# Splitting weights three tiles ahead in the last stage of a decoder layer

## The chip, the core and the metric

The kernel runs on one core of a Trainium2 chip. The metric is the time of one execution on the device, in microseconds (us), median of the runs shown. PE is the matrix engine, PEld its weight loads, DVE the vector engine, ACT the scalar engine, POOL the GpSimd engine, and SP the engine whose queue issues most DMAs.

## The reference

One decoder layer for a prompt of 1024 tokens and 64 sample tokens (8 sequences of 8), width 1024, all in fp32: a feed-forward half, a mixing part (forgetting attention beside gated linear attention), and a second feed-forward half. Only the second feed-forward half matters here:

```python
def swiglu(x, w_gu, w_down):
    gate, up = jnp.split(x @ w_gu, 2, axis=-1)
    return (jax.nn.silu(gate) * up) @ w_down

def macaron_half(x, g_pre, w_gu, w_down, g_post):
    return x + 0.5 * rmsnorm(swiglu(rmsnorm(x, g_pre), w_gu, w_down), g_post)
```

The hidden width is 2752: 21 blocks of 128 and a tail of 64.

## The kernel before, in words

All 1088 tokens lie in columns, the model dimension on partitions (8 slices of 128). A matrix product in fp32 accuracy is made of three products in a faster format: each operand is split into a high part and a low remainder, and high x high, high x low and low x high are summed in PSUM. `split` makes the parts: ACT casts the source to the high part (L192), DVE subtracts it from the source to give the low part (L193). For weights the source is a raw tile of 128x1024 (or 128x512), and the parts are called `wh` and `wl`.

`Feed` brings the weights. It holds one list of requests in the order in which jobs use them. A request is loaded into a raw tile (`wr`, two buffers, L117), split into `wh` and `wl` (three buffers each, `NW` = 3), and handed to its job by `get`. `free` says that a job has used its tiles, and calls `pump`, which writes further splits and loads: the splits up to `freed + ahead` tiles, and `ahead` is `NW - 1` = 2 where no caller says otherwise. So while job j is written, the tiles of j and j+1 are split. `work` goes through the jobs: get, pump, run the job, free.

The second feed-forward half runs twice: once for the first 512 tokens, and then, as the last stage of the kernel, for the other 576 (Part `f3`, begun by the job `start5`). This last stage makes the hidden blocks 2 to 19 in groups of 4, 4, 4, 4 and 2 ("sevens"). For each hidden block, gate and up products together would be 8 quarter products (two column halves of tokens by two halves of the contraction, for gate and for up); they are made with 7, after Winograd's form of Strassen's method. Each quarter product is 4 slices x 3 matmuls of 288 columns, in one PSUM tile. The operands of the 7 are sums of gate and up weights, which `Sums.load` makes for each block: tiles x (`wx`), y, z (`wz`) and s4. DMAs bring the raw parts, and POOL makes three sums for x and y (L89) and one for s4 (L94). x, y, z and s4 are the four tiles of the block's four jobs (`job_seven`, i = 0 to 3), with 2, 2, 2 and 1 products. Tile y, s4 and one raw part live in the memory of the first 512 tokens' result, which must have been written out first (`old3`).

The products are evacuated from PSUM by ACT (the first of a block, L581) or DVE (L565): sums of products give gate and up. After a block, ACT applies silu (L574), DVE multiplies by up (L575), and ACT and DVE split the result into `hh` and `hl` (L577, L578). In the last block of a group these steps are done for each half of the tokens apart. Then come the group's four down products (L495), each with one tile of `in_wd`, evacuated by DVE (L505). PSUM gives the products three tiles (`mm`) and one more for every fourth of a block (`mx`).

Within the sevens the flag `kept` makes ACT and DVE keep the order in which the code writes their instructions; elsewhere the framework's scheduler may reorder. After the sevens come the last two hidden blocks and their down products ("last"), and the final norm.

Of the kernel before, what the change touches and what calls it, by code (L numbers as in the profile page):

```python
# [31 lines left out]
NW = 3  # L32
# [35 lines left out]
class Sums:  # L68


    def __init__(self, gate, up, f, first=None):
        self.gate, self.up, self.f = gate, up, f
        self.i = 0 if first is None else first.count
        self.first = first or self
        self.first.count = self.i + 1
# [22 lines left out]
class Feed:  # L98


    def __init__(self, step, reqs):
        self.step, self.reqs = step, reqs
        self.raws, self.parts = [], []
        self.taken = self.freed = 0

    def _raw(self):
        s, nc = self.step, self.step.nc
        req = self.reqs[len(self.raws)]
        if isinstance(req, Sums):
            self.raws.append(req.load(s))  # L110
            return
        t = s.W.tile([P, KB * P], F32, name=s.uid("wr"), tag="wraw", bufs=NRAWW)
        pieces, _ = req
        o = 0
        for p in pieces:
            n = p.shape[-1]
            nc.sync.dma_start(t[:, o:o + n], p)  # L117
            o += n
        self.raws.append((t, o))
# [14 lines left out]
        s.split(hi[:, :n], lo[:, :n], t[:, :n])  # L134
        self.parts.append((hi, lo))

    def pump(self, ahead=NW - 1):
        while len(self.parts) < min(len(self.reqs), self.freed + ahead):
            self._split()
        while len(self.raws) < min(len(self.reqs), len(self.parts) + NRAWW):  # L140
            self._raw()
        while len(self.raws) < min(len(self.reqs), len(self.parts) + NSUMS) and isinstance(self.reqs[len(self.raws)], Sums):
            self._raw()
# [4 lines left out]
        self.taken += 1  # L148
        return self.parts[self.taken - 1]

    def free(self, n=1, ahead=NW - 1):
        self.freed += n
        self.pump(ahead)

# [989 lines left out]
class StepB(StepA):  # L1144
# [423 lines left out]
    def whole(self):  # L1568
# [158 lines left out]

        def start5():
            p4.close()
            f3.H, _ = self.pool("H2", keep=True)  # L1730
            self.px, _ = self.pool("px", keep=True, space=PSUM)
        norm0 = self.norm(y, 0, *CH[0], F, pre=0, key="f1", v=[self.rms_quick(y, CH[0][1], F)])
        next(norm0)
        jobs.append(([], start5, 0))
        jobs += self.ffn(A["wgu2"], A["wd2"], f3)
        self.work(jobs)
# [96 lines left out]
```

## Time and profile before

| | us |
|---|---|
| median of 3 runs | 2414.66 (2413.93 to 2417.48) |
| profiled execution | 2405.93 |
| its span, first to last instruction | 2404.2 |
| PE busy | 2300.9 (96%) |
| DVE, ACT, POOL busy | 1282.9, 899.8, 474.7 |

The mean granted clock of the matrix engine was 0.985 of full speed. In the span, the last stage with its first blocks starts near 1965 us; the first product of the sevens runs at 2004.5, the last near 2330, and the rest is the last two blocks and the norm.

How the rows read: in order of time, a row gives start, duration, engine, line, operation, output<-inputs, shape and count, and in brackets how long the engine sat idle before it and what ended that. A row of stretches gives for each engine the busy time, and then the granted clock, the share of the DMA engines and GB/s. Busy times of merged rows overlap, since instructions are pipelined.

### The profile page before, as it was taken

To read this page: it belongs to the slowest core of one execution; us is meant where nothing else is said; L and a number is where in the kernel's file an instruction comes from. 1 tells how busy PE (TensorE), PEld (TensorE's weight loads), DVE (VectorE), ACT (ScalarE), POOL (GpSimd) and SP (SyncE) were. 2 spreads that over 40 slices of the span, in tenths; PEclk is the share of its full clock that TensorE was granted. 3 is DMA by queue.
4 is the path that set the end of the run, shared out by engine and by line. 5 is a ranking of instruction groups with operands and counts; after the bars stand their busy time and mean duration, and the time that the engine had idled before them with its cause. 6 is when DMAs were issued, how large, how long until landed. Compare 5 with 4: busy or idle time off the path is not lost. (4 is left out here: it accounts for less than half of the span.)

```text
span 2404.2 us, 39346 instructions
## 1 busy us (share of the span) xinstructions
PE 2300.9 (96%) x15200; PEld 2041.1 (85%) x15200; DVE 1282.9 (53%) x2453; ACT 899.8 (37%) x1622; POOL 474.7 (20%) x514
## 2 busy tenths in 40 slices
PE   7999999999999999999998999999997999999997
PEld 7999999999989879899996666677777998999997
DVE  7223232232347775776464333358885786667655
ACT  5411211111134555755454212236465544333322
POOL 4000000000003230011134454611100324223302
PEclk9999999999999999999999999999998999999998
DMA  3211111111135577664458998755654534222212
GB/s 123 71 44 45 44 45 44 46 49 48 45 97 158 165 226 210 183 189 144 125 185 280 321 332 291 252 159 165 167 167 142 183 117 155 86 86 91 77 53 91
DMA packets 182268, 330.55 MB, mean 137 GB/s; under 512 B 25730, under 2 KB 101315, under 8 KB 182083
## 3 DMA queue, kind: packets, MB, share of 16 engines
q1 hardware_dynamic: 170418, 289.77, 38.7%
q0 software_dynamic: 11664, 38.28, 4.6%
q8 instruction: 120, 1.97, 0.3%
q14 instruction: 66, 0.53, 0.1%
HBM read 284.29 MB, written 43.69 MB: 136 GB/s over the span
## 5 line engine op out<-in xcount | busy, mean ns | idle before, releaser
L263 PE MATMUL mm<-ua,wh 128*128 128x512 f32 (+2 forms) x2288 | 636.6, 365 | 4.8 <-ACT ua L405 2.0
L263 PE MATMUL mm<-ub,wh 128*128 128x256 f32 (+2 forms) x2624 | 544.9, 303 | 10.4 <-ACT ub L192 8.0
L193 DVE TENSOR_TENSOR wl<-wr,wh 128x1024 fp32r<-128x1024 f32 (+1 forms) x258 | 312.6, 1212 | 339.4 <-ACT wh L192 337.4
L192 ACT CAST wh<-wr 128x1024 fp32r<-128x1024 f32 (+1 forms) x258 | 263.4, 1022 | 573.0 <-PE mm L263 220.7
L263 PEld LDWEIGHTS mm<-ua,wh 128*128 128x128 f32 (+1 forms) x2288 | 401.4, 192 | 80.8 <-issue 22.4
L263 PEld LDWEIGHTS mm<-ub,wh 128*128 128x128 f32 (+1 forms) x2624 | 427.2, 191 | 17.6 <-ACT ub L192 8.2
L263 PE MATMUL mm<-ua,wl 128*128 128x512 f32 (+1 forms) x1136 | 406.3, 359 | 0.9 <-DVE wl L193 0.9
L263 PE MATMUL mm<-ub,wl 128*128 128x256 f32 (+1 forms) x1296 | 385.9, 298 | 0.3 <-DVE wl L193 0.3
L495 PE MATMUL mm<-hl,wh 128*128 128x256 f32 (+2 forms) x1088 | 346.9, 320 | 0.0
L495 PE MATMUL mm<-hh,wh 128*128 128x256 f32 (+2 forms) x1040 | 336.9, 325 | 7.9 <-ACT wh L192 4.3
L495 PE MATMUL mm<-hh,wl 128*128 128x256 f32 (+2 forms) x1040 | 331.7, 320 | 2.1 <-DVE wl L193 2.1
L263 PEld LDWEIGHTS mm<-ub,wl 128*128 128x128 f32 x1296 | 247.7, 191 | 0.5 <-DVE wl L193 0.5
L263 PEld LDWEIGHTS mm<-ua,wl 128*128 128x128 f32 x1136 | 217.2, 192 | 33.0 <-DVE wl L193 2.0
L505 DVE TENSOR_TENSOR y<-y,mm 128x256 f32<-128x256 f32 (+2 forms) x272 | 130.3, 504 | 192.6 <-PE mm L495 191.5
L495 PEld LDWEIGHTS mm<-hh,wh 128*128 128x128 f32 x1040 | 196.0, 189 | 26.9 <-issue 6.2
L495 PEld LDWEIGHTS mm<-hl,wh 128*128 128x128 f32 x1088 | 206.0, 189 | 12.6 <-issue 1.3
L277 POOL TENSOR_TENSOR ss<-ss,sq 128x256 f32<-128x256 f32 (+1 forms) x46 | 46.2, 1005 | 834.1 <-ACT sq L273 833.5
L495 PEld LDWEIGHTS mm<-hh,wl 128*128 128x128 f32 x1040 | 196.1, 189 | 15.2 <-DVE wl L193 3.1
L961 POOL DMA_INDIRECT pr<-in_cv,rows x128 | 128.5, 1004 | 114.6 <-PE po L1038 60.2
L433 DVE TENSOR_TENSOR sg<-mm,sg 128x256 f32<-128x256 f32 (+4 forms) x76 | 39.3, 517 | 132.7 <-PE mm L263 130.7
L192 ACT CAST hh<-sg 128x512 fp32r<-128x512 f32 (+2 forms) x92 | 47.0, 511 | 156.3 <-DVE sg L433 134.4
L550 PE MATMUL mm<-ub,wh 128*128 128x288 f32 x432 | 89.0, 297 | 3.9 <-ACT y L503 3.9
(290 smaller groups left out, 3187.8 us busy)
## 6 DMA issues: line engine op xcount, KB each, us to landing
wr<-in_wgu SPq DMA_DIRECT2D x101, 512.0 KB
wr<-in_wd SPq DMA_DIRECT2D x60, 512.0 KB
pr<-in_ck SPq DMA_DIRECT2D x112, 256.0 KB
wr<-in_win SPq DMA_DIRECT2D x50, 512.0 KB
wr<-in_wout SPq DMA_DIRECT2D x32, 512.0 KB
wz<-in_wgu SPq DMA_DIRECT2D x36, 256.0 KB
h<-y SPq DMA_DIRECT2D x12, 512.0 KB
x<-h SPq DMA_DIRECT2D x24, 256.0 KB
```

The lines of the kernel that those rows point to most:

```text
L192: self.keep(self.nc.scalar.copy(hi, src))
L193: self.keep(self.nc.vector.tensor_tensor(out=lo, in0=src, in1=hi.bitcast(F32), op=ALU.subtract))
L263: nc.tensor.matmul(out, a, x[:, k, o:o + n], start=(k == 0 and j == 0), stop=(k == KB - 1 and j == len(ops) - 1))
L277: (nc.gpsimd if odd else nc.vector).tensor_tensor(out=s, in0=s, in1=sq[:, :n], op=ALU.add)
L433: nc.vector.tensor_tensor(out=out, in0=u, in1=t, op=ALU.mult)
L495: nc.tensor.matmul(pds[e], a, b, start=(i == 0 and j == 0), stop=(i == len(g) - 1 and j == len(ops) - 1))
L505: nc.vector.tensor_tensor(out=yk, in0=yk, in1=pds[e], op=ALU.add)
L550: nc.tensor.matmul(ps, a, x, start=(k == 0 and j == 0), stop=(k == KB // 2 - 1 and j == len(ops) - 1))
L961: nc.gpsimd.indirect_dma_start(out=raw[:, i], out_offset=None, in_=A["ck" if kind == "K" else "cv"].rearrange("g p n -> (g p) n"), in_offs ...
```

## The change

`Feed` gets a field `ahead`, 2 at first. `pump` and `free` use it where the caller gives no number. `start5` sets it to 3, so that from the last stage on the splits reach three tiles ahead: while job j is written, tile j+2 is split as well, into the buffers that job j-1 used.

```diff
@@ class Feed
         self.taken = self.freed = 0
+        self.ahead = NW - 1
...
-    def pump(self, ahead=NW - 1):
+    def pump(self, ahead=None):
+        ahead = ahead or self.ahead
         while len(self.parts) < min(len(self.reqs), self.freed + ahead):
             self._split()
...
-    def free(self, n=1, ahead=NW - 1):
+    def free(self, n=1, ahead=None):
         self.freed += n
         self.pump(ahead)
...
         def start5():
             p4.close()
+            self.feed.ahead = NW
```

It changes the order of instructions on each engine, and their number on none. Lines of the changed kernel are higher by 1 to 3.

DVE, second block of a group, before (`y<-y,mm` with number 20621 evacuates the block's second product, `wl<-wz` is the split of tile z, `wl<-y` with 128x512 that of s4, `wl<-y` with 128x1024 that of y):

```order
L565 TENSOR_TENSOR sg_20477<-y_7670,mm_20579 128x288
L193 TENSOR_TENSOR wl_20594<-y_7670,wh_20593 128x1024
L565 TENSOR_TENSOR y_7670<-y_7670,mm_20621 128x288
L575 TENSOR_TENSOR sg_20477<-sg_20477,up_20478 128x576
L193 TENSOR_TENSOR wl_20639<-wz_20461,wh_20638 128x1024
L565 TENSOR_TENSOR y_7670<-y_7670,mm_20642 128x288
L565 TENSOR_TENSOR y_7670<-y_7670,mx_20655 128x288
L565 TENSOR_TENSOR up_20607<-y_7670,mx_20655 128x288
L578 TENSOR_TENSOR hl_20470<-sg_20477,hh_20469 128x576
L193 TENSOR_TENSOR wl_20674<-y_7670,wh_20673 128x512
L565 TENSOR_TENSOR sg_20606<-y_7670,mm_20678 128x288
L565 TENSOR_TENSOR up_20607<-y_7670,mm_20691 128x288
```

The same place now:

```order
L567 TENSOR_TENSOR sg_20481<-y_7670,mm_20592 128x288
L195 TENSOR_TENSOR wl_20607<-wz_20430,wh_20606 128x1024
L567 TENSOR_TENSOR y_7670<-y_7670,mm_20625 128x288
L577 TENSOR_TENSOR sg_20481<-sg_20481,up_20482 128x576
L195 TENSOR_TENSOR wl_20643<-y_7670,wh_20642 128x512
L567 TENSOR_TENSOR y_7670<-y_7670,mm_20647 128x288
L567 TENSOR_TENSOR y_7670<-y_7670,mx_20660 128x288
L567 TENSOR_TENSOR up_20611<-y_7670,mx_20660 128x288
L580 TENSOR_TENSOR hl_20474<-sg_20481,hh_20473 128x576
L195 TENSOR_TENSOR wl_20679<-wx_20583,wh_20678 128x1024
L567 TENSOR_TENSOR sg_20610<-y_7670,mm_20682 128x288
L567 TENSOR_TENSOR up_20611<-y_7670,mm_20695 128x288
```

In each of the four slots for a split now stands the split of the next tile: z where y stood, s4 where z stood, the next block's x where s4 stood.

ACT, end of a group, before (`wh<-wr` are the casts of the group's first and second down weights, `sg<-sg` the silu of each half, `hh<-sg` the casts of the gated halves):

```order
L192 CAST wh_20928<-y_7670 128x512
L574 ACTIVATE sg_20859<-sg_20859 128x288
L577 CAST hh_20475<-sg_20859 128x288
L192 CAST wh_20966<-wr_20895 128x1024
L574 ACTIVATE sg_20859<-sg_20859 128x288
L577 CAST hh_20475<-sg_20859 128x288
L192 CAST wh_20990<-wr_20932 128x1024
```

The same place now:

```order
L194 CAST wh_20897<-y_7670 128x512
L579 CAST hh_20477<-sg_20741 128x576
L194 CAST wh_20934<-wr_20863 128x1024
L576 ACTIVATE sg_20865<-sg_20865 128x288
L579 CAST hh_20479<-sg_20865 128x288
L194 CAST wh_20972<-wr_20901 128x1024
L576 ACTIVATE sg_20865<-sg_20865 128x288
L579 CAST hh_20479<-sg_20865 128x288
```

Each cast of down weights moved ahead of the silu and the cast of one half. DVE's halves of these splits moved in the same way: that of the second down weights now stands ahead of the evacuation of the stage's last product.

SP's queue at the stage's start, before (`x<-h` and `out_yT<-y` belong to the output of the first 512 tokens, `y<-in_wgu` is a raw part for the first block's sums):

```order
L117 DMA wr_20271<-in_wd 128x512
L366 DMA x_24239<-h_87 128x2x320
L386 DMA out_yT<-y_7670 128x4x256
L366 DMA x_24241<-h_87 128x2x320
L386 DMA out_yT<-y_7670 128x4x256
L86 DMA y_7670<-in_wgu 128x512
L117 DMA wr_20895<-in_wd 128x1024
L117 DMA wr_20932<-in_wd 128x1024
```

The same place now:

```order
L118 DMA wr_20275<-in_wd 128x512
L118 DMA wr_20863<-in_wd 128x1024
L368 DMA x_24239<-h_87 128x2x320
L388 DMA out_yT<-y_7670 128x4x256
L368 DMA x_24241<-h_87 128x2x320
L388 DMA out_yT<-y_7670 128x4x256
L86 DMA y_7670<-in_wgu 128x512
L118 DMA wr_20901<-in_wd 128x1024
```

The first load of down weights (512 KB) moved ahead of the outputs and of the raw part. On POOL, the sum that completes y and the one that completes x have changed places in most blocks: y's is now second of the three, and x's third.

## The prediction

> **What bounds the kernel now.** I read the page first, then the table of waits from the stage with seven products to the end, then PE, DVE, ACT and POOL in order of time over one group of four blocks. In that stretch PE is nearly always busy, and no DMA holds it; what PE loses, it loses in small waits on weights that are not split yet. The table of waits (engine, line, tile, releaser: total us, times, longest):
>
> ```profile
> PE mm L550 <- DVE wl L193: 5.1, 11, 0.5
> PE mm L495 <- ACT wh L192: 4.3, 5, 1.0
> PE mm L550 <- ACT y L503: 3.9, 1, 3.9
> PE mm L495 <- DVE wl L193: 2.1, 4, 0.5
> ...
> PEld mm L550 <- DVE wl L193: 10.1, 20, 0.8
> ```
>
> The first and last row are the same stalls seen at PE and at its weight load: about 20 places where a product waits for the low half of its weights. Rows two and four are the four group ends (and the last one), where the down product waits for its first weights. The 3.9 is the start of the stage and happens once.
>
> How much that is per block, from the groups. ACT copies the first product of each block out of PSUM (L581), so these four rows are a clock for the blocks of the second group; the PE rows show the undisturbed pace and the two stalls of one block:
>
> ```profile
> 2083.05 0.40 ACT L581 COPY y<-mm 128x288 f32<-128x288 f32 x1 [7.05 <-PE mm L550]
> 2094.33 0.40 ACT L581 COPY y<-mm 128x288 f32<-128x288 f32 x1 [2.38 <-PE mm L550]
> 2106.57 0.40 ACT L581 COPY y<-mm 128x288 f32<-128x288 f32 x1 [2.52 <-PE mm L550]
> 2118.74 0.40 ACT L581 COPY y<-mm 128x288 f32<-128x288 f32 x1 [2.52 <-PE mm L550]
> ```
> ```profile
> 2094.13 0.42 PE L550 MATMUL mm<-ua,wh 128*128 128x288 f32 x2
> 2094.39 0.30 PE L550 MATMUL mm<-ua,wl 128*128 128x288 f32 x1
> 2094.53 0.43 PE L550 MATMUL mm<-ua,wh 128*128 128x288 f32 x2
> ...
> 2098.93 0.43 PE L550 MATMUL mm<-ub,wh 128*128 128x288 f32 x2
> 2099.86 0.40 PE L550 MATMUL mm<-ub,wl 128*128 128x288 f32 x1 [0.51 <-DVE wl L193]
> 2100.10 0.43 PE L550 MATMUL mm<-ub,wh 128*128 128x288 f32 x2
> ...
> 2104.47 0.42 PE L550 MATMUL mm<-ub,wh 128*128 128x288 f32 x2
> 2104.93 0.40 PE L550 MATMUL mm<-ub,wl 128*128 128x288 f32 x1
> ```
>
> Three matmuls take 0.40 us (2094.13 to 2094.53), so the 84 of a block (7 products of 4x3) need 11.2. Blocks one to two are 11.28 apart, two to three 12.24, three to four 12.17. The excess of 1.0 is two stalls: the low half of the third tile (z) comes 0.66 late (the third matmul is due 0.27 after 2098.93, and starts at 2099.86) and costs 0.1 more at the next matmul (0.24 instead of 0.13); the low half of the next block's first tile (x) comes 0.19 late at 2104.93, with 0.1 behind it.
>
> Why the halves are late:
>
> ```profile
> 2095.98 0.46 DVE L565 TENSOR_TENSOR y<-y,mm 128x288 f32<-128x288 f32 x1 [1.77 <-PE mm L550]
> 2096.35 1.22 DVE L575 TENSOR_TENSOR sg<-sg,up 128x576 f32<-128x576 f32 x1
> 2097.49 2.31 DVE L193 TENSOR_TENSOR wl<-wz,wh 128x1024 fp32r<-128x1024 f32 x1
> ...
> 2322.57 0.75 DVE L575 TENSOR_TENSOR sg<-sg,up 128x576 f32<-128x576 f32 x1
> 2323.24 1.22 DVE L193 TENSOR_TENSOR wl<-wz,wh 128x1024 fp32r<-128x1024 f32 x1
> ```
> ```profile
> 2094.29 1.29 POOL L89 TENSOR_TENSOR y<-y,wz 128x512 f32<-128x512 f32 x1 [3.60 <-DVE wl L193]
> 2095.66 1.29 POOL L89 TENSOR_TENSOR wx<-y,wx 128x512 f32<-128x512 f32 x1
> 2096.92 1.81 POOL L89 TENSOR_TENSOR y<-wx,y 128x512 f32<-128x512 f32 x1
> ```
>
> On DVE the z split stands behind the evacuation of the product before it, which waits for PE until 2095.98, and behind the gating multiply. From there to the end of the split is 3.8 us, and PE gives it 3.2 (two products). Beside POOL's three sums for the next block the multiply takes 1.22 and the split 2.31; in the last block, where POOL has nothing to do, 0.75 and 1.22, and there is no stall.
>
> **The change, part by part.** It adds and removes no instruction. From the stage's start each split is written one tile earlier, so on ACT and DVE it stands ahead of one more product's evacuation.
>
> *A, within the groups.* Removable, per group of four: 0.08, 1.04, 0.97 and, in the fourth block, the z stall alone, 0.7: 2.8. Four groups: 11.2; the group of two loses 0.1. Does the new order fit? I lay the new DVE rows against a block that starts at 0, with products ending every 1.6, and today's durations, contention included. The z split of this block ends by 3.5 and is due at 6.4. The evacuation of the second product and the multiply end at 5.0, the s4 split at 5.7 (due 9.6), three evacuations at 7.2, the low half of the gated product at 7.9, the next block's x split, whose buffer is free at 6.4, at 9.1 (due 11.2), two evacuations at 10.0, the y split at 12.0 (buffer free at 9.6; due 14.4), the last evacuation at 12.4 (its PSUM tile is due at 14.4). The smallest slack is about 2 us; today it is below nothing. DVE's load fits too, but barely:
>
> ```profile
> 2094.13:2106.38 12.25, 10.01 (x14) 1.00 0.29 88
> ```
>
> It is 10.0 busy of 12.25 now and 10.0 of 11.2 then. I count A as 11, all of it (ends: 1, if DVE becomes the bound, see below, and 11.3).
>
> *B, group ends.* PE around the second one, with ACT's rows:
>
> ```profile
> 2128.68 0.29 PE L550 MATMUL mm<-ub,wl 128*128 128x288 f32 x1
> 2129.92 0.39 PE L495 MATMUL mm<-hh,wh 128*128 128x256 f32 x1 [0.95 <-ACT wh L192]
> ...
> 2130.38 0.28 PE L495 MATMUL mm<-hl,wh 128*128 128x256 f32 x1
> 2131.18 0.38 PE L495 MATMUL mm<-hh,wl 128*128 128x256 f32 x1 [0.52 <-DVE wl L193]
> ```
> ```profile
> 2127.10 0.44 ACT L574 ACTIVATE sg<-sg 128x288 f32<-128x288 f32 x1 [3.96 <-DVE sg L565]
> 2128.49 0.43 ACT L577 CAST hh<-sg 128x288 fp32r<-128x288 f32 x1 [0.94 <-DVE sg L575]
> 2128.83 1.04 ACT L192 CAST wh<-wr 128x1024 fp32r<-128x1024 f32 x1
> ```
>
> The cast of the first down weights stands behind the silu and cast of the first half of the gated product. PE is 1.11 late at 2129.92 and 0.68 at 2131.18, each with 0.1 behind it: 2.0 per group end, 8.0 over four. In the new order that cast stands ahead of the silu, with a buffer that is free 4.8 us before the stage's last product ends, so both stalls go. What is late next: the second down weights' split now stands ahead of the last product's evacuation on DVE, and behind the first half's cast. By the same durations that evacuation ends at 13.7 on the block's clock, where the down product needs its PSUM tile at 14.1 (24 matmuls of 0.12 after 11.2). That is 0.4 of slack; one slower split eats it. I take 7 (ends: 2, if 1.5 per group comes back there, and 8).
>
> *C, the start.* Two rows set it:
>
> ```profile
> 1999.41 1.29 POOL L89 TENSOR_TENSOR y<-y,wz 128x512 f32<-128x512 f32 x1 [5.30 <-DMA y<-in_wgu]
> 2004.54 0.78 PE L550 MATMUL mm<-ub,wh 128*128 128x288 f32 x2 [3.94 <-ACT y L503]
> ...
> 1992.83 0.69 DVE L193 TENSOR_TENSOR wl<-wr,wh 128x512 fp32r<-128x512 f32 x1
> ```
>
> PE waits for POOL's sums, and these for a load into memory that the output of the stage before must leave first. In the new order a 0.69 split moves up into the vector work that makes that output, and on SP's queue a 512 KB weight load moves ahead of that output's DMA and of this load. The split costs 0.7 one for one; the load's bytes, 2.9 us apart where such loads follow one another (tail, below), cost between 0 and 2.9. One ACT copy no longer waits behind the first cast, worth at most the 0.4 of a copy. Ends: +0.4 and -3.6; I take -1, near the split, since the bytes only move ahead of the output's and are not added.
>
> *D, the tail.* The last down products and the last blocks are paced by loads:
>
> ```profile
> 2340.45 1.05 ACT L192 CAST wh<-wr 128x1024 fp32r<-128x1024 f32 x1 [2.26 <-DMA wr<-in_wgu]
> 2343.30 1.05 ACT L192 CAST wh<-wr 128x1024 fp32r<-128x1024 f32 x1 [1.80 <-DMA wr<-in_wgu]
> ...
> 2343.21 0.38 PE L495 MATMUL mm<-hh,wh 128*128 128x256 f32 x1 [1.04 <-DVE y L505]
> ```
>
> Loads land 2.85 apart, and PE's evacuations wait on DVE behind a split that waits for one. Splitting earlier starts the chain somewhat earlier, but puts one more load-bound split ahead of evacuations. The 0.8 gained at the last group's end is given back here; I count 0, with ends of -1 and +1.3 (the whole stall of 2343.21).
>
> Sum: 11 + 7 - 1 + 0 = 17 us off. The profiled execution took 2405.93 us (span 2404.2); the median of the runs, 2414.66, stands 8.7 above it, without anything in the trace to say where. Off the median: **2397.7**.
>
> **Rivals.** R1: the group ends stay. The place is the evacuation with 0.4 of slack in B. If it costs 1.2 to 1.5 per group, B is 2 and the gain 12: 2402.7. For it: DVE is crowded there; against it: POOL is idle at a group's end, and splits take their short 1.22 then.
>
> R2: DVE becomes the bound. The new order makes other splits run beside POOL's sums. If the x and y splits too take 2.31 for 1.22, DVE needs 10.0 + 2 x 1.09 = 12.2 per block, as long as a block is now; A is then about 0 to 1, the gain 6 to 7: 2408. For it: two of the DVE rows above already double beside POOL. Against it: the sums are three per block whenever they run, so what they slow should move, not multiply: the y split that releases them ends as they start, and the x split comes 3 us after they end. The Trainium skill speaks for R2 ("SBUF — State Buffer", section "Who interferes with whom"): a DVE instruction with two SBUF inputs contends with a GpSimd instruction that reads SBUF, and the later one is blocked until the other is done. The trace agrees in direction with its 2.31 against 1.22; by the rule at its worst, one block per sum, the time would be R2's, by my sum it is 17 off.
>
> R3, the other sign: the raw sums come too late. In the new order x's sum is POOL's third of three instead of its second for most blocks, and its split is due one tile earlier. The chain from the end of the y split (0.8 into the block) is 1.3 + 1.8 + 1.3 on POOL, 1.05 on ACT and 1.4 on DVE: 6.9, and there are 10.4 until the next block starts. From a chain of 10.4 PE waits; from about 12 the wait per block exceeds today's 1.0 and what the group ends give (0.6 per block), and the kernel is slower, since ACT and DVE run in order and the evacuations queue behind. At 13 it would be some 13 blocks x 1: about 2424 with C. Against it are 3.5 us of margin.
>
> R4: nothing happens, because the split, earlier in the order, still waits for the buffer that the last product has just left. Then 2414.7. Against it: on the clock of A every buffer is free 4.8 to 6.4 us before its split's result is due.
>
> **How the numbers follow.** The forecast has 0.60, R1 0.17, R2 0.13 (half of it within 0.2%, that is 4.8 us, about what a measurement of this kernel can tell), R3 0.07, R4 0.03. Faster: 0.60 + 0.17 + 0.07 = 0.84; same 0.06 + 0.03 = 0.09; slower 0.07. The range takes in the best ends (11.3 + 8 + 1.3 + 0.4 = 21: 2393.7) and R2's 2408: 2393.5 to 2409. Outside it remain R3, R4, a piece of R2 and a gain beyond the best ends, 0.16 together.
>
> **What would show it.** Right: L581 rows 11.2 to 11.3 apart in all blocks; the waits of L550 on wl under 1 us in all; first down matmul within 0.2 of the last product at a group's end; the start's gap 0.5 to 2 longer. Wrong: DVE without idle time before L565 rows and splits of 2.3 on x or y (R2); a wait of a down matmul on the evacuation L565 (R1); ACT's cast of wx waiting for POOL (R3).

## The result: 0.9914 of the time before, and the profile after

The changed kernel takes 2394.43 us, median of 6 runs (2390.86 to 2398.61), against 2415.23 for the kernel before in the same comparison: a ratio of 0.9914, 95% interval 0.9901 to 0.9928. The forecast was 2397.7 and the range 2393.5 to 2409. A second comparison gave 0.9930 (0.9916 to 0.9945, below); what both intervals hold is 0.9916 to 0.9928, 17 to 20 us. One of the six runs of the second comparison took 3178.46 us at a granted clock of 0.652 and is not in its ratio.

The profiled execution of the changed kernel took 2397.51 us (span 2395.8). First the table of waits of PE and its weight load from the stage's start to the end (us in total, times, longest):

```profile
PE mm L552 <- ACT wh L194: 4.1, 1, 4.1
...
PE mm L497 <- DVE y L507: 1.7, 2, 1.1
PE mm L497 <- DVE sg L567: 1.0, 5, 0.3
...
PE mm L497 <- DVE hl L195: 0.5, 1, 0.5
```

The eleven waits of the seven products (now L552) on the low halves `wl`, 20 at the weight load, are gone without a rest, and so are the waits of the down products (L497) on `wh` and `wl` at the group ends. The wait of 4.1 is the stage's start, 3.9 before. Two rows are new: at all five group ends a down product waits up to 0.3 for an evacuation, L567, and once, at the start, 0.5 for the low half of a hidden block (`hl`, L195).

ACT's copies of each block's first product, the clock that the prediction used:

```profile
2089.43 0.40 ACT L583 COPY y<-mm 128x288 f32<-128x288 f32 x1 [0.70 <-PE mm L552]
2100.61 0.40 ACT L583 COPY y<-mm 128x288 f32<-128x288 f32 x1 [0.67 <-PE mm L552]
2111.78 0.40 ACT L583 COPY y<-mm 128x288 f32<-128x288 f32 x1 [0.68 <-PE mm L552]
2122.95 0.40 ACT L583 COPY y<-mm 128x288 f32<-128x288 f32 x1 [0.67 <-PE mm L552]
```

They stand 11.18, 11.17 and 11.17 apart; before, 11.28, 12.24 and 12.17. DVE over most of one block, the order that the diff announced:

```profile
2107.49 1.22 DVE L195 TENSOR_TENSOR wl<-wx,wh 128x1024 fp32r<-128x1024 f32 x1
...
2109.60 1.22 DVE L195 TENSOR_TENSOR wl<-y,wh 128x1024 fp32r<-128x1024 f32 x1 [0.16 <-ACT wh L194]
2110.74 0.45 DVE L567 TENSOR_TENSOR sg<-y,mm 128x288 f32<-128x288 f32 x1
2111.14 2.14 DVE L195 TENSOR_TENSOR wl<-wz,wh 128x1024 fp32r<-128x1024 f32 x1
2113.43 0.46 DVE L567 TENSOR_TENSOR y<-y,mm 128x288 f32<-128x288 f32 x1 [0.15 <-PE mm L552]
2113.80 1.25 DVE L577 TENSOR_TENSOR sg<-sg,up 128x576 f32<-128x576 f32 x1
2114.97 1.78 DVE L195 TENSOR_TENSOR wl<-y,wh 128x512 fp32r<-128x512 f32 x1
```

The z split now starts at 2111.14, ahead of the evacuation at 2113.43, and no longer behind it. It ends at 2113.28. The copy at 2111.78 follows the end of its block's first product by 0.2, so that product began near 2110.0. The fifth product, the first to need z, is due four products of 1.6 after that, at about 2116.4: 3.1 to spare (2.9 in the schedule of the prediction), where 0.66 were missing.

For the rest, the last stage is cut at PE's own marks in each trace, and from here on "stage" means what lies behind the first of these marks: the first blocks' down products (from the first `mm<-hh,wt`) up to the first of the seven products (start, with its gap), then for each group the time from its first product to its first down product (blocks), and from there to the next group (down). Worked out from the starts of PE's rows, in us:

| kernel | start | blocks of groups 1, 2, 3, 4, 5 | down after groups 1, 2, 3, 4, 5 | stage to the end |
|---|---|---|---|---|
| before | 16.91 | 50.22, 48.67, 48.69, 48.69, 23.14 | 26.49, 26.48, 26.48, 27.21, 15.17 | 416.5 |
| after | 17.78 | 47.71, 44.69, 44.69, 44.69, 22.35 | 26.04, 26.14, 26.05, 26.04, 15.12 | 399.6 |

The stage is 16.9 shorter, and this is the change's worth in this pair of traces. What the first comparison shows beyond that is put down to scatter of the code ahead of the stage: PE's instructions up to there stand in the same order in both traces. The first mark in three executions (before, after, after again):

```profile
1987.63 0.36 PE L495 MATMUL mm<-hh,wt 128*128 128x256 f32 x1
```
```profile
1996.10 0.36 PE L497 MATMUL mm<-hh,wt 128*128 128x256 f32 x1
```
```profile
2000.46 0.36 PE L497 MATMUL mm<-hh,wt 128*128 128x256 f32 x1
```

The same instruction comes 8.5 and 12.8 us later. The profiled execution of before has the shortest way to the stage of all traces here. That is in line with the 8.7 us by which it stood below its median, left unexplained in the prediction; with one trace of that kernel it isn't shown.

### The profile page after: what moved, and what is told of

Its sections match the earlier page's. It is cut to its first block, busy times and chain, and to the rows that moved or that the text cites. A ratio compares the mean times of both kernels' runs of the same rounds, so it can differ in the third digit from the quotient of the medians.

```text
span 2395.8 us, 39346 instructions
## 1 busy us (share of the span) xinstructions
PE 2297.4 (96%) x15200; PEld 2041.2 (85%) x15200; DVE 1293.7 (54%) x2453; ACT 903.4 (38%) x1622; POOL 488.2 (20%) x514
## 5 line engine op out<-in xcount | busy, mean ns | idle before, releaser
L265 PE MATMUL mm<-ub,wh 128*128 128x256 f32 (+2 forms) x2624 | 546.2, 303 | 10.7 <-ACT ub L194 8.3
L195 DVE TENSOR_TENSOR wl<-wr,wh 128x1024 fp32r<-128x1024 f32 (+1 forms) x258 | 312.0, 1210 | 337.7 <-ACT wh L194 325.7
L497 PE MATMUL mm<-hl,wh 128*128 128x256 f32 (+2 forms) x1088 | 347.2, 320 | 0.8 <-DVE hl L195 0.5
L497 PE MATMUL mm<-hh,wh 128*128 128x256 f32 (+2 forms) x1040 | 337.1, 325 | 4.1 <-DVE y L507 2.0
L497 PE MATMUL mm<-hh,wl 128*128 128x256 f32 (+2 forms) x1040 | 331.9, 320 | 1.0 <-issue 1.0
L497 PEld LDWEIGHTS mm<-hl,wh 128*128 128x128 f32 x1088 | 205.9, 189 | 13.8 <-issue 2.0
L279 POOL TENSOR_TENSOR ss<-ss,sq 128x256 f32<-128x256 f32 (+1 forms) x46 | 46.1, 1003 | 836.9 <-ACT sq L275 836.3
L497 PEld LDWEIGHTS mm<-hh,wh 128*128 128x128 f32 x1040 | 196.0, 189 | 23.3 <-issue 6.5
L497 PEld LDWEIGHTS mm<-hh,wl 128*128 128x128 f32 x1040 | 196.4, 189 | 12.7 <-issue 1.1
L552 PE MATMUL mm<-ub,wh 128*128 128x288 f32 x432 | 88.5, 298 | 4.1 <-ACT wh L194 4.1
```

The costliest lines, as they stand in the source:

```text
L195: self.keep(self.nc.vector.tensor_tensor(out=lo, in0=src, in1=hi.bitcast(F32), op=ALU.subtract))
L265: nc.tensor.matmul(out, a, x[:, k, o:o + n], start=(k == 0 and j == 0), stop=(k == KB - 1 and j == len(ops) - 1))
L279: (nc.gpsimd if odd else nc.vector).tensor_tensor(out=s, in0=s, in1=sq[:, :n], op=ALU.add)
L497: nc.tensor.matmul(pds[e], a, b, start=(i == 0 and j == 0), stop=(i == len(g) - 1 and j == len(ops) - 1))
L552: nc.tensor.matmul(ps, a, x, start=(k == 0 and j == 0), stop=(k == KB // 2 - 1 and j == len(ops) - 1))
```

## Experiments

Each kernel ran beside the kernel before on one chip; the first four share their runs of before (median 2414.09), the last four theirs (2411.96). What decides is the table of stage lengths, since it leaves the scatter ahead of the stage out. It has scatter of its own, from stretches at a lower clock: up to some 3 us at the stage's start (under C below), and 1.5 us at a time at some group ends (under blocks only).

| kernel | ratio of times (95%) | start | blocks of groups 1 to 5 | down after groups 1 to 5 | stage |
|---|---|---|---|---|---|
| after again | 0.9930 (0.9916 to 0.9945) | 17.95 | 47.13, 44.69, 44.69, 44.69, 22.35 | 26.04, 26.11, 26.05, 26.04, 15.04 | 399.1 |
| blocks only | 0.9949 (0.9936 to 0.9962) | 18.18 | 45.90, 45.79, 45.80, 45.80, 23.03 | 26.49, 27.97, 26.48, 26.72, 14.89 | 405.4 |
| ends only | 0.9971 (0.9958 to 0.9983) | 16.76 | 50.59, 47.59, 47.57, 47.58, 22.45 | 26.41, 26.41, 26.41, 26.41, 15.35 | 411.8 |
| late start | 0.9925 (0.9912 to 0.9938) | 16.92 | 47.86, 44.69, 44.69, 44.69, 22.34 | 26.05, 26.14, 26.04, 26.05, 15.12 | 398.9 |
| ends fixed | 0.9913 (0.9893 to 0.9933) | 16.77 | 47.00, 44.69, 44.69, 44.69, 22.34 | 25.60, 25.60, 25.59, 25.60, 13.94 | 394.8 |
| ends and tail | 0.9902 (0.9885 to 0.9920) | 17.07 | 46.56, 44.70, 44.69, 44.69, 22.34 | 25.59, 25.59, 25.60, 25.60, 13.45 | 393.7 |
| no sums | 0.9961 (0.9946 to 0.9976) | 14.51 | 46.23, 46.11, 46.12, 46.13, 23.13 | 31.91, 26.48, 27.97, 26.55, 15.20 | 408.8 |
| three everywhere | 0.9966 (0.9951 to 0.9981) | 17.10 | 45.62, 44.69, 44.69, 44.69, 22.34 | 26.04, 26.04, 26.04, 26.04, 14.71 | 396.3 |

**After again.** The changed kernel once more, as a measure for the others.

> The changed kernel once more, to see how far the whole time and the stages repeat. In the traces the last stage (first down product of its first blocks to the end) is 16.9 us shorter than before, while the timed medians differ by 20.8. Theory (the change works in the last stage alone): the last stage again takes 396.2 to 396.5 us in the profile, the full groups' sevens 44.7 each, and the timed gain comes nearer to 17 than to 21. Rival (something ahead of the stage is faster too): the timed gain stays at 20 or more.

The stage repeats within 0.5 us (it is 399.1 after 399.6; the 396.2 to 396.5 that was expected does not fit this cut), and the ratio is worth 16.9 us of 2414.09. The stage's saving and this ratio agree; the first comparison's 20.8 was 4 more.

**Blocks only.** The sums (x, y, z, s4) are split three ahead, the down weights two ahead as before.

```diff
+    def lead(self, ahead):
+        sums = isinstance(self.reqs[min(len(self.parts), len(self.reqs) - 1)], Sums)
+        return NW - 1 if self.ahead == NW and not sums else ahead
...
-        while len(self.parts) < min(len(self.reqs), self.freed + ahead):
+        while len(self.parts) < min(len(self.reqs), self.freed + self.lead(ahead)):
```

> Only the sum tiles (x, y, z, s4) are split three ahead, the down weights two ahead as before. Theory (two separate gains, A in the blocks and B at the group ends): a full group's sevens take 45.8 us up to the first down product (44.7 in the changed kernel, 48.7 before), because the first down product again waits 1.1 for its weights; the down products take 26.5; the start does not get longer; in sum 11 us faster than before, about 6 slower than the changed kernel. Rival (one gain: whoever is ahead in the blocks is ahead at the ends): 44.7 and no loss against the changed kernel.

Groups 2 to 4 go from 48.68 to 45.80: term A is 2.88 per group, against the 2.8 of the prediction. What is left over 44.69 is the first stall of a group end, and both of these stand where they stood (PE, end of the first group):

```profile
2062.76 0.39 PE L501 MATMUL mm<-hh,wh 128*128 128x256 f32 x1 [0.94 <-ACT wh L198]
2064.02 0.39 PE L501 MATMUL mm<-hh,wl 128*128 128x256 f32 x1 [0.53 <-DVE wl L199]
```

Two things did not come as expected. The start got longer, 18.18, with a down product in it that waits 2.82 for an evacuation on ACT, which before doesn't have. And the down products after group 2 take 27.97 instead of 26.48, without a new wait of PE: right behind the two stalls the granted clock (the number behind POOL's pair) drops for some 3.4 us.

```profile
2136.00:2140.00 4.00, 3.70 (x20) 3.70 (x21) 1.82 (x5) 1.82 (x3) 0.00 (x0) 0.64 0.45 131
```

That costs 1.5, at one group end of four here and at none in the trace of before.

**Ends only.** The other half: down weights three ahead from the first of the seven products, sums two ahead.

```diff
-        return NW - 1 if self.ahead == NW and not sums else ahead
+        return NW - 1 if sums else ahead
```

> Only the down weights are split three ahead (from the first block with seven products on), the sum tiles two ahead as before. Theory: blocks stay 12.2 apart within a group, a full group's sevens take 47.5 us, the down products 26.0, and the kernel is 7 to 8 us faster than before; with the 11 of the run with the sum tiles alone that adds up to the whole gain plus the 0.9 lost at the start. Rival (the ends gain only where the blocks do): under 3 us faster.

Blocks lose their first end stall (48.68 to 47.58, 1.10) and keep the z and x stalls. The second end stall is replaced. Its table of waits, and the down product in question:

```profile
PE mm L556 <- DVE wl L199: 5.6, 12, 0.5
...
PE mm L501 <- DVE sg L572: 2.4, 5, 0.6
```
```profile
2070.27 0.28 PE L501 MATMUL mm<-hh,wl 128*128 128x256 f32 x1
2071.11 0.41 PE L501 MATMUL mm<-hh,wh 128*128 128x320 f32 x1 [0.56 <-DVE sg L572]
```

The 320-column part of the first down product, due 0.12 behind the row above it, is 0.72 late for the evacuation L572, and the table has five such waits. That takes back what the second stall cost, so the down products take 26.41 and not the 26.0 that was expected, and the stage gains 4.7 where 7 to 8 were expected. The two halves are still separate gains, 11.1 and 4.7 in the stage; with 15.8 their sum is within 2 of the whole, and without the 1.5 of the clock in blocks only it would be 17.3.

**Late start.** Three ahead begins with the first job of the seven products instead of `start5`.

```diff
@@ start5
-            self.feed.ahead = NW
@@ job_seven
+            if i == 0:
+                self.feed.ahead = NW
```

> The changed kernel, but three ahead begins only in the first job with seven products, so that no weight load and no split move into the output of the first 512 tokens. Theory (the changed kernel loses 0.9 us there): the stretch from the first down product of the first blocks to the first of the seven products takes 16.9 us instead of 17.8, all else as in the changed kernel: 0.5 to 1.5 us faster than it, which the trace can tell and the timing hardly. Rival (the 0.9 is the scatter of that stretch): 17.8 again.

The start is back at 16.92, 0.86 to 1.03 less than in the two runs of the change: that much of term C is shown. The first group keeps its 3.2 over the others (47.86 against 44.69), so that part isn't made by the early split.

**Ends fixed.** As late start, and in the last block of a group the second down weights' split is written behind the last product's evacuation again, and three ahead goes on after it.

```diff
                 seven(z, w, 1, "t4", second)
+                if last:
+                    self.feed.ahead = NW - 1
...
                     add(t[:, b], z.u, ps)
                     if last:
+                        self.feed.ahead = NW
+                        self.feed.pump()
```

> As late_start, and in the last block of a group the split of the second down weights is written behind the evacuation of the last product instead of ahead of it. Theory (the 0.45 that a group's first down product still loses at its second column part is that evacuation, waiting on DVE behind that split): the down products of a full group take 25.5 to 25.6 us instead of 26.05, the last stage 397 us instead of 398.9, that is 2 us less. Rival (the 0.45 is the halves of the gated product): 26.05 again.

The new stall goes at all four group ends, 26.05 to 25.60. DVE at the second of them, in the changed kernel and here:

```profile
2133.99 1.23 DVE L195 TENSOR_TENSOR wl<-wr,wh 128x1024 fp32r<-128x1024 f32 x1 [0.49 <-ACT wh L194]
2135.14 0.45 DVE L567 TENSOR_TENSOR sg<-y,mm 128x288 f32<-128x288 f32 x1
```
```profile
2132.71 0.45 DVE L569 TENSOR_TENSOR sg<-y,mm 128x288 f32<-128x288 f32 x1
2133.28 1.23 DVE L195 TENSOR_TENSOR wl<-wr,wh 128x1024 fp32r<-128x1024 f32 x1
```

Above, the evacuation waits behind the split, and this in turn for ACT's cast behind the first half of the gated product; below, the evacuation is through first, and PE runs on (the changed kernel's PE, then this one's):

```profile
2135.08 0.28 PE L497 MATMUL mm<-hh,wl 128*128 128x256 f32 x1
2135.64 0.41 PE L497 MATMUL mm<-hh,wh 128*128 128x320 f32 x1 [0.28 <-DVE sg L567]
```
```profile
2134.37 0.28 PE L497 MATMUL mm<-hh,wl 128*128 128x256 f32 x1
2134.49 0.31 PE L497 MATMUL mm<-hh,wh 128*128 128x320 f32 x1
```

0.56 from one to the next against 0.12: 0.44 per group end.

**Ends and tail.** As ends fixed, and back to two ahead in the down products of the last group, where splits wait for loads.

```diff
+            if f.room and len(g) == 2 and HB_TAIL not in g:
+                self.feed.ahead = NW - 1
+                self.flush()
```

> As ends_fixed, and for the last group's down products the splits go back to two ahead and stand behind the evacuations. Theory (the 1.3 us stall in these down products is evacuations waiting on DVE behind a split that waits for a load): they take 13.7 to 13.9 us instead of 15.1, and the last stage gets about 1.2 us shorter than in ends_fixed. Rival (the loads themselves pace this place): the wait moves to the next blocks' first weights, and nothing is gained.

The last group's down products take 13.45, 1.7 less than in the changed kernel; 1.2 of that had come with ends fixed, where the stall of 1.1 in these products (under D below) is gone already. So this edit doesn't test its own theory, and why the stall went with ends fixed was not traced. Ends and tail has the shortest stage and the lowest ratio of all: 5.9 us ahead of the changed kernel in the stage, of which 1.2 is a shorter first group, which no edit here sets (below). The times alone don't separate the two (0.9902 against 0.9914 and 0.9930, with intervals that overlap).

**No sums.** The kernel before, with POOL's three sums for x and y left out: the halves of x and y are loaded instead, so the last stage's results aren't the reference's. It asks whether DVE's long splits, and with them the z stall, come from POOL.

```diff
-            for out, a, b, op in ((y[:, lo], a21, z[:, hi], ALU.add), ...
-                nc.gpsimd.tensor_tensor(out=out, in0=a, in1=b, op=op)
+            for t, src in ((y[:, lo], self.up[:, lo]), (x[:, hi], self.gate[:, hi]), (y[:, hi], self.up[:, hi])):
+                nc.sync.dma_start(t, src)
```

> The kernel before (splits two ahead), with POOL's three sums per block left out: the parts that they would make are loaded from the weights instead, so the results of the last stage are not the reference's, and its timing is. Theory (the z stall of 0.77 per block comes from DVE's multiply and z split being slowed beside POOL's sums): multiply 0.75 and z split 1.22 in all blocks, blocks 11.5 apart instead of 12.2, a full group's sevens 46.3 to 46.5 us instead of 48.7, the group ends unchanged. Rival (the order alone makes the stall): blocks stay 12.2 apart.

DVE's groups over 43 us of the second group, before and here (busy us, mean ns):

```profile
L193 DVE TENSOR_TENSOR wl<-wz,wh 128x1024 fp32r<-128x1024 f32 x4 | 8.2, 2040 | 0.0
```
```profile
L192 DVE TENSOR_TENSOR wl<-wz,wh 128x1024 fp32r<-128x1024 f32 x4 | 4.9, 1218 | 0.0
L574 DVE TENSOR_TENSOR sg<-sg,up 128x576 f32<-128x576 f32 x3 | 2.3, 751 | 0.0
```

Without POOL beside it the z split takes 1.22 and the multiply 0.75, and with the order of before the blocks shrink from 48.7 to 46.1, with no wait for a low half left in them. Of the 1.4 left over 44.69, 1.1 is the first stall of a group end. So POOL's sums are what makes the z split late; the change removes by order what could also go with its cause. The group ends were expected unchanged, but after groups 1 and 3 the down products take 31.91 and 27.97. After group 3 that is the low clock of blocks only again, 1.5 behind the two stalls. After group 1 it comes twice, the second time behind a new wait of 2.15 for an evacuation (L504), whose cause was not traced. So the time gains less than the blocks.

**Three everywhere.** Three ahead from the kernel's first split on.

```diff
-        self.ahead = NW - 1
+        self.ahead = NW
```

> Three ahead in the whole kernel instead of the last stage alone. Theory (a gain comes only where PE waits for splits, and outside the last stage such waits sum to some 5 us): within 5 us of the changed kernel, either way, and the last stage as in the changed kernel. Rival (the deeper splits also hold up evacuations in other stages): more than 5 us slower than the changed kernel.

The stage is as short as the change makes it, 396.3, but it begins only at 2013.8, later than in any other trace (1987.6 to 2000.5). Of the 20 us that the stage saves, the ratio of 0.9966 leaves 8 (5 to 12 by its interval), so about 12 are lost ahead of it. The same product of the mixing part, before, after and here:

```profile
1682.14 0.40 PE L1404 MATMUL go<-qe,S 128*128 128x16 f32 x2
```
```profile
1692.21 0.40 PE L1406 MATMUL go<-qe,S 128*128 128x16 f32 x2
```
```profile
1710.87 0.51 PE L1406 MATMUL go<-qe,S 128*128 128x16 f32 x3
```

The loss is there already: 18.7 against after, of which 1.0 is there at 1018 and 16.2 at 1392 in after's time. The longest wait of PE between them that after doesn't have is this one:

```profile
PE mm L497 <- DVE wt L640: 4.1, 1, 4.1
```

PE's order of instructions, the same in before and after up to the stage, is another here from about 878 us on, since the scheduler may reorder outside the sevens. How the loss comes about was not traced, and stays open.

## Why the prediction was right

The total was right: 17 off forecast, 16.9 in the stage. The time of 2394.43 owes some 4 us of its distance from before to the scatter ahead of the stage and lies only 0.9 above the lower end of the range. By its own terms, with the differences of the tables:

| term | predicted | measured | from |
|---|---|---|---|
| A, within groups | 11 | 11.6 | 4 x 2.88, and 0.1 in group 5 (blocks only) |
| B, four group ends | 7 | 6.8 | first stall 4 x 1.11; down 0.45, 0.34, 0.43, 1.17 |
| C, start | -1 | -2.4 | 0.87 in the start, 1.5 in the first group |
| D, tail | 0 | 0.7 | group 5: blocks 0.68, down 0.05 |

The terms miss by +0.6, -0.2, -1.4 and +0.7, which cancel to -0.3; that the sum came out this close is in part luck.

**A** held with its mechanism. Its premise on DVE did not quite. The prediction said that what POOL's sums slow should move and not multiply. It moved and grew: beyond the unhindered 1.22, 0.75 and 0.69 the z split, the multiply and the s4 split of the block shown take 0.92, 0.50 and 1.09, 2.5 together, where before the z split and multiply lost 1.6 and s4 nothing. DVE in the stretch of one block, after:

```profile
2100.40:2111.57 11.17, 11.17 (x86) 11.17 (x85) 10.70 (x14) 5.44 (x7) 6.54 (x5) 1.00 0.26 96
```

It is 10.7 busy of 11.17 (the third pair of numbers), not 10.0, while PE (the first) is busy throughout. **R2** was thus nearer than the 10.0 let it seem: about 0.5 more per block would have made DVE the bound. It did not come, as the x and y splits kept their 1.22 and only what ran beside the three sums was stretched. The Trainium skill's rule ("SBUF — State Buffer", section "Who interferes with whom") agrees in direction with POOL's own rows too:

```profile
2112.15 2.28 POOL L89 TENSOR_TENSOR y<-wx,y 128x512 f32<-128x512 f32 x1
2114.40 1.81 POOL L89 TENSOR_TENSOR wx<-y,wx 128x512 f32<-128x512 f32 x1
```

They take 1.3 undisturbed and are stretched together with DVE's. R2's time, which by the prediction the rule would give at its worst, did not come.

**B** had the right size with a piece of luck. The place named as next late, the last evacuation behind the second down weights' split, was late indeed: R1's place, at 0.44 per group instead of its 1.2 to 1.5. Ends fixed shows it. The 0.4 of slack laid out was in truth -0.3, 0.1 of the loss being the restart. Against that, the down products of the fourth group gained 1.17, because one wait on an evacuation that they had before was absent; with the 0.43 of the third group in its place B is 6.1. That wait, before:

```profile
2289.25 0.39 PE L495 MATMUL mm<-hh,wh 128*128 128x256 f32 x1 [0.48 <-DVE y L505]
```

**C** is the term mis-sized. The split moved ahead costs 0.87, near the 1 that was taken, though not where the prediction looked for it: the gap grew by 0.2 only (3.94 to 4.12), where 0.5 to 2 was the sign, and 0.45 of it is a new wait of a down product ahead of the gap, for the low half of the hidden block on DVE.

```profile
2002.02 0.42 PE L497 MATMUL mm<-hl,wh 128*128 128x320 f32 x1 [0.45 <-DVE hl L195]
```

The other 1.5 is in the first group's blocks, for which the prediction had no term: 3.0 over the other groups, 1.5 before. After the gap PE runs on a lower clock for a while. The granted clock is the number behind POOL's pair; stretches after the gap, before and after:

```profile
2004.00:2008.00 4.00, 3.30 (x12) 2.95 (x13) 2.45 (x2) 2.08 (x5) 1.71 (x2) 0.58 0.68 234
2008.00:2012.00 4.00, 4.00 (x32) 4.00 (x31) 1.96 (x2) 1.97 (x3) 2.61 (x3) 0.99 0.01 4
```
```profile
2012.00:2016.00 4.00, 2.02 (x7) 1.67 (x8) 2.14 (x2) 3.21 (x5) 2.02 (x2) 0.63 0.23 66
2016.00:2020.00 4.00, 4.00 (x19) 4.00 (x19) 1.45 (x2) 0.77 (x3) 3.53 (x3) 0.52 0.54 181
```

Before, the low clock is over by 2008, 3.5 after the first product; after, it lasts until 2019.8, 5.9 after. The first group's excess is 2.4 in after again, 3.2 in late start (a gap of 3.9, as before), 1.9 in ends and tail (4.1): it varies from run to run after nearly the same gap, and no edit sets it. The Trainium skill says so too ("TensorE: Matmul & The Clock Gate", section "What's actually happening"): the window that decides runs freely, so the length depends on where the restart falls. The traces agree, with 3.5 and 5.9 after gaps of 3.94 and 4.12.

**D** was a sum of a gain at the last group's end and its return in the tail. The gain came (0.68); the return did not, since the tail kept its length and its stall of before:

```profile
2336.42 0.42 PE L497 MATMUL mm<-hh,wh 128*128 128x320 f32 x1 [1.10 <-DVE y L507]
```

**R3** and **R4** did not occur. R3's sign was the shown wait of ACT's cast of wx on POOL: there is one in the stage, at its start, inside the gap, and none in the blocks:

```profile
ACT wh L194 <- POOL wx L89: 4.1, 1, 4.1
```

R3's price was summed too low: 13 blocks at 1 and the 1 of C, on 2414.7, make about 2429 and not 2424.

## What to carry to other kernels

Where engines run their instructions in written order, look at what stands ahead of a late instruction, not only at how long it takes: a split moved ahead of an evacuation that waits for the matrix engine turned a stall of 0.7 per block into slack, with no instruction less. Then lay the new order out against the measured durations to the place that is late next; here it named the stall that was left (0.44 per group end), and moving that one instruction back removed it. Make the lead a matter of the stage: the same lead everywhere gave back more than half of the gain.

## What the runs showed of the hardware that was not expected

Vector and POOL instructions that overlap stretch each other and don't only change places in the queue: 1.78 instead of 0.69 for a 128x512 subtraction, 2.28 instead of 1.3 for a POOL sum, and with the new order DVE's loss per block rose from 1.6 to 2.5 us. After a gap of some 4 us the granted clock of the matrix engine was low for a while, and the first group of blocks took between 1.5 and 3.2 us longer than the later ones, in before, after, ends only, late start, ends fixed and ends and tail. A low clock also came behind short stalls: of the 12 group ends with stalls of 0.95 and 0.52 within 1.3 us (four each in before, blocks only and no sums), three were followed by a low clock for 3.4 us, worth 1.5 each. In the blocks and down products of the ten traces the low clock comes nowhere else before the final norm, except behind the start's gap and behind the wait of 2.15 in no sums. So a stall can cost more than its own length, and not every time. And the same code ahead of the stage took between 1987.6 and 2000.5 us, more than half of the effect under study, so a stage's length cut at the same instructions tells more than one profile's total.
